# A hybrid decoder layer on one core: the FFN chunk's epilogue in four steps instead of three, and the order of the last down projection

## The chip, the cores and the metric

One NeuronCore of a Trainium2 chip runs the whole program in one launch. The metric is the device time of one execution in microseconds (us); for the kernel before it is 1596.26 us, the median of three runs (1596.19 to 1596.4).

## The reference, cut to what matters

One layer with a model width of 2048 over 256 tokens, in float32: a hybrid mixer, then the FFN on which the change works, then a last norm. D_FF is 5632.

```
h = h + hybrid_mixer(rms_norm(h, norm_mix), ...)
u = rms_norm(h, norm_ffn)
h = h + (silu(u @ w_gate) * (u @ w_up)) @ w_down      # 2048 -> 5632 -> 2048
return rms_norm(h, norm_final)
```

## The kernel before, in words

**Matmuls in halves.** Every float32 operand is cut into a high and a low part by `split` (L107 on ACT makes the high part, L108 on DVE subtracts it from the value), and every product is three matmuls (high by high, low by high, high by low). So each 2048-column piece of a weight costs ACT one activation and DVE one subtraction before PE may use it.

**Units, and who sets the order.** The order is written out by hand: the program issues instructions in the order in which Python runs, and each engine works its own queue in that order. `run` goes through a list of units. For unit j it first issues the cuts (`split`) and the weight loads of units some places ahead, bounded by a count of buffers (`cap`), then `unit.multiply()`, then the unit's epilogue if it is the last of its group (`g.after`), and then it advances `clock` by one and lets `step_side` resume one side job. A side job is a generator: `beside(gen, after, lag)` sets its first step `after` ticks ahead, and after each `yield` it sleeps `lag` ticks. All that a step issues stands in the engines' queues between the matmuls of unit j and those of unit j + 1.

**The FFN's chunks.** D_FF is worked in 11 chunks of 512 columns, in four parts: `PARTS` is (0,3), (3,6), (6,9), (9,11). A chunk (`swiglu`) computes the gate and the up product together in 11 units, in the order N, N, Wp, Ws, N, Wp, Ws, N, Wp, Ws, N. An N unit is 24 matmuls of 512 columns, Wp 9 and Ws 12. All are of line L381. The products are summed in seven PSUM banks (of eight), from which VectorE puts the four results together (`squares_early` after the last Ws, L388 to L390; `squares_end`, L397 to L401). The cut of a Wp also makes four sums on DVE (L363 to L365).

**The chunk's epilogue** is the side job `finish`. It has three steps. Step 1: `squares_end` and two silu activations on ACT (L872). Step 2: two multiplications on DVE (L875, one per 128 tokens) that make act, then four transposes of act on PE (L881, each 128 by 128, into one fresh bank), and the `split` of that bank into the slot `act[f]`. Step 3: the other four transposes into another bank, and their `split`. For a chunk that is not the last of its part `after` is 2, so step 1 stands behind the first unit of the next chunk (N), step 2 behind the second (N) and step 3 behind the third (Wp). For the last chunk of a part `after` is 1: step 1 stands right behind its own last unit, and step 2 and step 3 behind the first two units of the down projection.

**The down projection** follows each part: `down(part, n)` for four groups of 512 output columns. A unit is a K-tile of one chunk's 512 rows, 24 matmuls (L275, L276, L280), so a group has as many units as the part has chunks. It accumulates in two banks. Groups put together in a tuple are interleaved by `in_order`: first all their units but the last one, then the last units. In all parts the first two groups are such a tuple. The last unit of a group uses the part's last chunk. The last part also scales by the final norm (`after`, L916 to L919) and its fourth group is staggered: its two units are worked per token tile, and `final_norm` writes out.

Of the kernel before, what the change touches and what calls it, by code (L numbers as in the profile page):

```python
# [17 lines left out]
D_MODEL = 2048  # L18
# [14 lines left out]
CH = 512  # L33
# [17 lines left out]
def trunk(ctx: ExitStack, tc: tile.TileContext, x, norm_mix, norm_ffn, w_in, w_pool, pool_scale,  # L51
# [19 lines left out]
    def name(s):  # L71
        uid[0] += 1
        return f"{s}_{uid[0]}"

    def slot(shape, dt=F32):
        return slots.tile([P] + shape, dt, tag="slot", name=name("slot"))
# [15 lines left out]
    def bank():  # L92
        return psum.tile([P, CH], F32, tag="bank", name=name("bank"))
# [4 lines left out]
    def cols(n):  # L98
        return slice(n * CH, (n + 1) * CH)
# [4 lines left out]
    def split(hi, lo, src, scale=None):  # L104

        if scale is None:
            nc.scalar.activation(hi, src, AF.Copy)  # L107
            nc.vector.tensor_tensor(lo, src, f32(hi), OP.subtract)  # L108
        else:
            nc.scalar.activation(hi, src, AF.Copy, scale=scale)  # L110
            nc.vector.scalar_tensor_tensor(lo, src, scale, f32(hi), OP.mult, OP.subtract)
# [61 lines left out]
    def square_sum(dst, src):  # L173
        nc.scalar.activation(wk(), src, AF.Square, accum_out=dst)
# [21 lines left out]
    def beside(gen, after=2, lag=2):  # L196
        side.append([clock[0] + after, lag, gen])
# [187 lines left out]
    def squares_early(b):  # L385

        c12, w, x = wk(), wk(), wk()
        nc.scalar.activation(c12, b[1], AF.Copy)  # L388
        nc.vector.tensor_tensor(w, b[6], c12, OP.subtract)
        nc.vector.tensor_tensor(x, b[7], w, OP.add)  # L390
        return c12, w, x

    def squares_end(b, early):

        c12, w, x = early
        c21 = wk()
        nc.vector.tensor_tensor(w, b[5], w, OP.add)  # L397
        nc.vector.tensor_tensor(c21, b[5], x, OP.add)
        nc.vector.tensor_tensor(w, b[3], w, OP.add)  # L399
        nc.vector.tensor_tensor(c12, b[2], c12, OP.add)  # L400
        nc.vector.tensor_tensor(x, b[4], x, OP.subtract)  # L401
        return (w, c12), (c21, x)
# [137 lines left out]
    def qkv(s, base, then):  # L540
        return ([heads_T("q" + s, base, c, HEAD_DIM ** -0.5, turned=s == "a") for c in range(2)]
                + [heads_T("k" + s, base + WIDTH, c, 1.0) for c in range(2)]
                + [tokens("v" + s, base + 2 * WIDTH, c, then if c else None) for c in range(2)])
# [153 lines left out]
    def pair(t):  # L697
        return t.rearrange("p (k s) -> p k s", k=2)
# [154 lines left out]
    def load_gf():  # L853
        gf.append(slot([D_MODEL]))
        nc.sync.dma_start(gf[0], bass.AP(tensor=norm_final.tensor, offset=norm_final.offset,
                                         ap=[[0, P], [1, D_MODEL]]))

    def swiglu(f, last):

        early = []  # L860

        def load(raw, p):
            for i, w in enumerate((w_gate, w_up)):
                nc.sync.dma_start(raw[:, :, i, :], w[2 * p * P:2 * (p + 1) * P, cols(f)].rearrange("(j p) c -> p j c", p=P))

        def begin(b):
            early.append(squares_early(b))

        def finish(b):
            c = squares_end(b, early[0])  # L870
            for t in range(NT):
                nc.scalar.activation(c[t][0], c[t][0], AF.Silu, scale=rstd2[t])  # L872
            yield
            for t in range(NT):
                nc.vector.scalar_tensor_tensor(c[t][1], c[t][1], rstd2[t], c[t][0], OP.mult, OP.mult)  # L875
            act[f] = a = slot([8, SEQ], F32R)
            for k in range(2):
                pt = bank()
                for i in range(2):
                    for t in range(NT):  # L880
                        nc.tensor.transpose(pt[:, i * SEQ + t * P:i * SEQ + (t + 1) * P],  # L881
                                            c[t][1][:, (2 * k + i) * P:(2 * k + i + 1) * P], ident)
                split(a[:, 2 * k:2 * k + 2, :], a[:, 4 + 2 * k:6 + 2 * k, :], pair(pt))
                if k == 0:
                    yield
            ready.add(f)

        def before():
            cap[0] = 9

        def after(b):
            beside(finish(b), after=1 if last else 2, lag=1)

        return Squares(lambda: hT[0], FFN_KINDS, load, after, begin, before)

    def down(part, n):
        f0, f1 = PARTS[part]
        last = part == len(PARTS) - 1
        cs = cols(n)

        def lhs():
            def tile(kt):
                assert kt // 4 in ready
                return act[kt // 4][:, kt % 4, :], act[kt // 4][:, 4 + kt % 4, :]
            return tile

        def before():
            if last and n == 0:
                load_gf()
                nc.scalar.preload_act_table(AF.Sqrt)  # L910

        def after(acc, t=None, c=slice(0, CH)):
            if t is not None:
                return final_norm(acc, t, c)
            for t in range(NT):
                nc.vector.tensor_add(h[t][:, cs], acc[t], h[t][:, cs])  # L916
                if last:
                    square_sum(st3[:, t, n:n + 1], h[t][:, cs])
                    nc.vector.tensor_mul(h[t][:, cs], h[t][:, cs], gf[0][:, cs])  # L919
            if last and n == 2:  # L920
                nc.vector.tensor_reduce(st3[:, :, 4], st3[:, :, 0:3], AX.X, OP.add)
                nc.vector.tensor_scalar(st3[:, :, 4], st3[:, :, 4], 1.0 / D_MODEL, EPS, OP.mult, OP.add)

        return Group(lhs, range(4 * f0, 4 * f1), w_down, f0 * CH, n * CH, after, before, staggered=last and n == 3,
                     span=4)

    def final_norm(acc, t, c):

        hc = h[t][:, 3 * CH + c.start:3 * CH + c.stop]
        a = [st3[:, t, k:k + 1] for k in range(10)]  # L930
        nc.vector.tensor_add(hc, acc[:, c], hc)
        nc.scalar.activation(wk()[:, c], hc, AF.Square, accum_out=a[3])
        nc.vector.tensor_mul(hc, hc, gf[0][:, 3 * CH + c.start:3 * CH + c.stop])
        if c.stop < CH:
            nc.vector.scalar_tensor_tensor(a[4], a[3], 1.0 / D_MODEL, a[4], OP.mult, OP.add)
            return
        nc.scalar.activation(a[6], a[3], AF.Sqrt, scale=1.0 / D_MODEL, bias=a[4])
        nc.vector.scalar_tensor_tensor(a[5], a[3], 1.0 / D_MODEL, a[4], OP.mult, OP.add)
        nc.vector.reciprocal(a[7], a[6])
        nc.vector.scalar_tensor_tensor(a[8], a[7], a[7], a[5], OP.mult, OP.mult)  # L940
        nc.vector.tensor_scalar(a[8], a[8], -0.5, 1.5, OP.mult, OP.add)
        nc.vector.tensor_mul(a[9], a[7], a[8])
        for n in (0, 1, 3, 2):
            hn = h[t][:, cols(n)]
            if n in (0, 3):
                nc.vector.tensor_scalar(hn, hn, a[9], None, OP.mult)
            else:
                nc.scalar.activation(hn, hn, AF.Copy, scale=a[9])
            nc.sync.dma_start(out[toks(t), cols(n)], hn)

    groups = qkv("a", 0, start_block)
# [5 lines left out]
    for part, (f0, f1) in enumerate(PARTS):  # L957
        for f in range(f0, f1):
            groups += [swiglu(f, f == f1 - 1)]
        groups += [(down(part, 0), down(part, 1)), down(part, 2), down(part, 3)]  # L960

    def first_norm():
        rstd_of(st1)
# [39 lines left out]
```

## Time and profile before

| | |
|---|---|
| median of three runs | 1596.26 us |
| the profiled execution's own time | 1599.63 us |
| its span, first to last instruction | 1597.9 us |
| mean granted TensorE clock | 0.993 |
| PE busy (matmuls) | 1563.4 us, 98% |
| PEld busy (weight loads) | 1332.2 us, 83% |
| DVE busy | 1000.1 us, 63% |
| ACT busy | 724.8 us, 45% |
| DMA | mean 188 GB/s |

The span is the time between the first and the last instruction of one profiled execution. PE and PEld are the two sides of TensorE: matmuls and the weight loads ahead of them. Where a row ends in square brackets, these hold the time for which the engine sat idle just before it, and what ended the wait. The matmuls of the FFN's first chunk begin at 850.3 us; from there to the end of the span chunks and down projections follow each other.

### The profile page before, as it was taken

The numbers are of one execution on the slowest core, as the hardware profiler recorded it, in microseconds if no ns is written. First come the engines' busy times: TensorE is split into PE (matmuls) and PEld (weight loads), VectorE is DVE, ScalarE is ACT, GpSimd is POOL, SyncE is SP. The second block draws the span as 40 slices with busy tenths as digits, with TensorE's granted clock in tenths as the row PEclk, the third lists the DMA queues.
The fourth block names the chain that finished last, engine by engine and source line by source line (L and its number), as shares of the span: only waits on it lengthen the run. The fifth ranks groups of instructions, "written<-read, shape, count | busy, mean of one in ns | idle before, by whom it ended". The sixth has DMA issues, their size and how long they took to land.

```text
span 1597.9 us, 19167 instructions
## 1 busy us (share of the span) xinstructions
PE 1563.4 (98%) x7921; PEld 1332.2 (83%) x7921; DVE 1000.1 (63%) x996; ACT 724.8 (45%) x754; POOL 26.4 (2%) x94
## 2 busy tenths in 40 slices
PE   8999999999999999999999899999999999999997
PEld 8998999988888888888888777888778887788876
DVE  6453664735464453644657788576885768857675
ACT  7324443445644344343555455343553445534453
POOL 2000000101000000000000000000000000000000
PEclk9999999999999999999999999999999999999999
DMA  9655454554555555567555456555565555755551
GB/s 344 211 185 181 148 167 158 191 176 140 190 193 197 183 187 185 184 209 252 175 181 181 162 183 237 163 179 186 183 237 168 176 187 182 236 185 174 195 211 53
DMA packets 152359, 300.12 MB, mean 188 GB/s; under 512 B 6432, under 2 KB 7504, under 8 KB 152144
## 3 DMA queue, kind: packets, MB, share of 16 engines
q1 hardware_dynamic: 151968, 297.84, 55.3%
q8 instruction: 62, 1.02, 0.3%
q0 software_dynamic: 304, 1.06, 0.2%
q14 instruction: 25, 0.20, 0.0%
HBM read 296.77 MB, written 2.11 MB: 187 GB/s over the span
## 4 chain that ended last, share of the span: by engine, by line
PE 86%; DVE 8%; ACT 3%; issue 2%; DMA 0%; ACTq 0%; SPq 0%; DVEq 0%
PE bank L381 19%; PE bank L275 17%; PE bank L276 17%; PE bank L280 16%; PE bank L295 5%; PE bank L297 5%; PE bank L303 5%; DVE slot L108 4%; ACT slot L107 2%; DVE wk L875 1%; PE bank L881 1%; DVE slot L363 1%; ACT wk L872 1%; DVE wk L399 0%; DVE wk L397 0%
## 5 line engine op out<-in xcount | busy, mean ns | idle before, releaser
L108 DVE TENSOR_TENSOR slot<-slot,slot 128x1024 fp32r<-128x1024 f32 (+3 forms) x459 | 700.6, 1563 | 277.7 <-ACT slot L107 277.7
L107 ACT ACTIVATE slot<-slot 128x1024 fp32r<-128x1024 f32 (+3 forms) x459 | 590.3, 1328 | 336.7 <-DVE slot L108 122.6
L275 PE MATMUL bank<-slot,slot 128*128 128x512 f32 (+1 forms) x1192 | 466.9, 392 | 0.0
L276 PE MATMUL bank<-slot,slot 128*128 128x512 f32 (+1 forms) x1192 | 464.4, 390 | 0.0
L280 PE MATMUL bank<-slot,slot 128*128 128x512 f32 (+1 forms) x1192 | 310.2, 388 | 0.0
L381 PE MATMUL bank<-slot,slot 128*128 128x512 f32 x1254 | 293.0, 393 | 0.0
L381 PEld LDWEIGHTS bank<-slot,slot 128*128 128x128 f32 x1254 | 235.5, 189 | 49.1 <-DVE slot L108 0.7
L275 PEld LDWEIGHTS bank<-slot,slot 128*128 128x128 f32 x1192 | 225.5, 189 | 45.7
L276 PEld LDWEIGHTS bank<-slot,slot 128*128 128x128 f32 x1192 | 225.5, 189 | 45.6
L280 PEld LDWEIGHTS bank<-slot,slot 128*128 128x128 f32 x1192 | 222.9, 188 | 46.0
L381 PE MATMUL bank<-slot,late 128*128 128x512 f32 x759 | 173.8, 389 | 0.0
L381 PEld LDWEIGHTS bank<-slot,late 128*128 128x128 f32 x759 | 142.5, 188 | 29.6
L295 PE MATMUL bank<-slot,slot 128*128 128x256 f32 x640 | 159.3, 287 | 0.2 <-ACT slot L107 0.2
L297 PE MATMUL bank<-slot,slot 128*128 128x256 f32 x640 | 157.5, 283 | 0.0
L295 PEld LDWEIGHTS bank<-slot,slot 128*128 128x128 f32 x640 | 123.2, 193 | 0.7 <-ACT slot L107 0.6
L297 PEld LDWEIGHTS bank<-slot,slot 128*128 128x128 f32 x640 | 123.3, 193 | 0.0
L107 ACT ACTIVATE slot<-bank 128x512 fp32r<-128x512 f32 (+1 forms) x46 | 23.2, 523 | 155.9 <-PE bank L881 80.6
L303 PE MATMUL bank<-slot,slot 128*128 128x256 f32 x640 | 89.8, 283 | 0.0
L303 PEld LDWEIGHTS bank<-slot,slot 128*128 128x128 f32 x640 | 82.6, 192 | 0.0
L108 DVE TENSOR_TENSOR slot<-bank,slot 128x512 fp32r<-128x512 f32 (+1 forms) x46 | 26.8, 596 | 60.8 <-ACT slot L107 60.8
L755 ACT ACTIVATE wk<-bank,st 128x512 f32<-128x512 f32 x24 | 15.2, 686 | 85.6 <-PE bank L280 85.6
L916 DVE TENSOR_TENSOR slot<-bank,slot 128x512 f32<-128x512 f32 x30 | 19.6, 686 | 44.7 <-PE bank L280 44.7
(156 smaller groups left out, 575.4 us busy)
## 6 DMA issues: line engine op xcount, KB each, us to landing
slot<-in_w_in_dram SPq DMA_DIRECT2D x103, 1024.0 KB, 5.1
slot<-in_w_gate_dram SPq DMA_DIRECT2D x88, 512.0 KB, 3.9
slot<-in_w_up_dram SPq DMA_DIRECT2D x88, 512.0 KB, 4.8
slot<-in_w_down_dram SPq DMA_DIRECT2D x44, 1024.0 KB, 5.1
slot<-in_w_out_dram SPq DMA_DIRECT2D x16, 1024.0 KB, 5.1
slot<-in_w_br_a_dram SPq DMA_DIRECT2D x8, 1024.0 KB, 5.1
slot<-in_w_br_b_dram SPq DMA_DIRECT2D x8, 1024.0 KB, 5.1
slot<-in_w_br_c_dram SPq DMA_DIRECT2D x8, 1024.0 KB, 5.1
```

The costliest lines, as they stand in the source:

```text
L107: nc.scalar.activation(hi, src, AF.Copy)
L108: nc.vector.tensor_tensor(lo, src, f32(hi), OP.subtract)
L275: nc.tensor.matmul(acc[:, c], hi[:, toks(t)], whi[:, j, c], start=i + j == 0, stop=False)
L276: nc.tensor.matmul(acc[:, c], lo[:, toks(t)], whi[:, j, c], start=False, stop=False)
L280: nc.tensor.matmul(acc[:, c], hi[:, toks(t)], wlo[:, j, c], start=False, stop=i + j == n - 1)
L295: nc.tensor.matmul(o, whi[:, j, w], hi, start=i + j == 0 and c % 2 == 0, stop=False, skip_group_check=True)
L297: nc.tensor.matmul(o, whi[:, j, w], lo, start=False, stop=False, skip_group_check=True)
L303: nc.tensor.matmul(o, wlo[:, j, w], hi, start=False, stop=i + j == n - 1 and c % 2 == 1, skip_group_check=True)
L363: nc.vector.tensor_tensor(s[:, 0:2], raw[:, 0:1].to_broadcast([P, 2, CH]), raw[:, 1:3], OP.add)
L381: nc.tensor.matmul(g.banks[b], x[:, s, :], w[:, k, :], start=start, stop=g.left[b] == 0)
L872: nc.scalar.activation(c[t][0], c[t][0], AF.Silu, scale=rstd2[t])
L916: nc.vector.tensor_add(h[t][:, cs], acc[t], h[t][:, cs])
```

## The change

A `yield` is put into `finish` between the two multiplications and the first transposes. The epilogue has four steps: `squares_end` and silu; the multiplications; four transposes with their split; the other four with theirs. With the lag of one tick both sets of transposes, the slot of act and the two splits stand one unit later in the queues. For a chunk inside a part they stand behind the third unit (Wp) and the fourth (Ws) of the next chunk, for the last chunk of a part behind the second and the third unit of the down projection.

In the last part, which has two chunks, three down groups instead of two are put in the tuple, so their order of units is group 0, 1, 2 of the first chunk, then group 0, 1, 2 of the second chunk, and then the staggered fourth group. In the parts of three chunks the order of units stays.

```
             for t in range(NT):
                 nc.vector.scalar_tensor_tensor(c[t][1], c[t][1], rstd2[t], c[t][0], OP.mult, OP.mult)
+            yield
             act[f] = a = slot([8, SEQ], F32R)
             for k in range(2):
                 pt = bank()
...
         for f in range(f0, f1):
             groups += [swiglu(f, f == f1 - 1)]
-        groups += [(down(part, 0), down(part, 1)), down(part, 2), down(part, 3)]
+        k = 2 if f1 - f0 > 2 else 3
+        groups += [tuple(down(part, n) for n in range(k))] + [down(part, n) for n in range(k, D_MODEL // CH)]
```

## Rows read from the trace of the kernel before

**Rows 1.** The page, part 1: busy time, share of the span, instructions per engine.

```profile
PE 1563.4 (98%) x7921; PEld 1332.2 (83%) x7921; DVE 1000.1 (63%) x996; ACT 724.8 (45%) x754; POOL 26.4 (2%) x94
```

**Rows 2.** Groups by line, PE, 890 to 1598: busy us, mean ns, idle before, releaser.

```profile
L381 PE MATMUL bank<-slot,slot 128*128 128x512 f32 x1140 | 266.0, 393 | 0.0
...
L881 PE MATMUL bank<-ident,wk 128*128 128x128 f32 x88 | 17.5, 304 | 19.0 <-DVE wk L875 19.0
```

**Rows 3.** Timeline of PE behind the first chunk: start, length, instructions, idle before.

```profile
908.40 0.47 PE L881 MATMUL bank<-ident,wk 128*128 128x128 f32 x1 [4.22 <-DVE wk L875]
909.06 0.90 PE L881 MATMUL bank<-ident,wk 128*128 128x128 f32 x3 [0.19 <-DVE wk L875]
909.61 4.19 PE L381 MATMUL bank<-slot,slot 128*128 128x512 f32 x9
913.60 1.05 PE L881 MATMUL bank<-ident,wk 128*128 128x128 f32 x4
```

**Rows 4.** Timeline of PE behind the second, the fourth and the fifth chunk.

```profile
954.88 0.33 PE L881 MATMUL bank<-ident,wk 128*128 128x128 f32 x1 [0.65 <-DVE wk L875]
955.55 0.55 PE L881 MATMUL bank<-ident,wk 128*128 128x128 f32 x3 [0.33 <-DVE wk L875]
955.85 2.32 PE L381 MATMUL bank<-slot,slot 128*128 128x512 f32 x9
958.00 0.60 PE L881 MATMUL bank<-ident,wk 128*128 128x128 f32 x4
...
1111.07 0.55 PE L881 MATMUL bank<-ident,wk 128*128 128x128 f32 x3 [0.33 <-DVE wk L875]
...
1154.41 0.33 PE L881 MATMUL bank<-ident,wk 128*128 128x128 f32 x1 [0.81 <-DVE wk L875]
```

**Rows 5.** Timeline of PE behind the third chunk, and the last.

```profile
994.89 0.33 PE L881 MATMUL bank<-ident,wk 128*128 128x128 f32 x1 [2.25 <-DVE wk L875]
...
1547.63 0.33 PE L881 MATMUL bank<-ident,wk 128*128 128x128 f32 x1 [2.25 <-DVE wk L875]
```

**Rows 6.** Stretches: length, busy of PE, PEld, DVE, ACT, POOL, then PEclk, DMA, GB/s.

```profile
996.00:1001.00 5.00, 5.00 (x17) 3.92 (x17) 2.98 (x2) 2.40 (x2) 0.00 (x0) 0.66 0.51 193
1195.00:1200.00 5.00, 4.89 (x17) 4.06 (x18) 2.21 (x3) 2.40 (x2) 0.00 (x0) 0.69 0.60 211
1394.00:1399.00 5.00, 4.67 (x23) 3.86 (x23) 2.56 (x3) 2.40 (x2) 0.00 (x0) 1.00 0.61 210
1548.00:1554.00 6.00, 5.70 (x20) 4.59 (x21) 3.23 (x3) 2.40 (x2) 0.00 (x0) 0.72 0.01 3
...
908.00:914.00 6.00, 5.42 (x15) 4.14 (x16) 1.70 (x3) 0.60 (x1) 0.00 (x0) 0.50 0.08 12
...
1113.90:1155.40 41.50, 40.35 (x182) 33.00 (x179) 36.84 (x30) 21.44 (x15) 0.00 (x0) 1.00 0.60 203
```

**Rows 7.** Timeline of PE and DVE in the last down projection.

```profile
1553.95 2.00 PE L280 MATMUL bank<-slot,slot 128*128 128x512 f32 x8
...
1557.06 0.69 DVE L108 TENSOR_TENSOR slot<-bank,slot 128x512 fp32r<-128x512 f32 x1 [3.46 <-ACT slot L107]
...
1559.89 1.98 PE L280 MATMUL bank<-slot,slot 128*128 128x512 f32 x8
...
1565.33 1.98 PE L280 MATMUL bank<-slot,slot 128*128 128x512 f32 x8
```

**Rows 8.** Timeline of DVE and ACT behind the fourth chunk.

```profile
1109.60 1.41 DVE L875 SCALAR_TENSOR_TENSOR wk<-wk,st,wk 128x512 f32<-128x512 f32 x2
...
1111.71 0.60 ACT L107 ACTIVATE slot<-bank 128x512 fp32r<-128x512 f32 x1 [4.35 <-PE bank L881]
1112.34 0.69 DVE L108 TENSOR_TENSOR slot<-bank,slot 128x512 fp32r<-128x512 f32 x1 [1.33 <-ACT slot L107]
...
1115.40 1.22 DVE L363 TENSOR_TENSOR slot<-slot 128x1024 f32<-128x1024 f32 x1
...
1120.11 4.49 DVE L108 TENSOR_TENSOR slot<-slot,slot 128x2048 fp32r<-128x2048 f32 x2 [0.38 <-ACT slot L107]
```

More of the change, by code (lines that the diff above doesn't have):

```diff
@@ L875, in finish @@
                 nc.vector.scalar_tensor_tensor(c[t][1], c[t][1], rstd2[t], c[t][0], OP.mult, OP.mult)
+            yield
             act[f] = a = slot([8, SEQ], F32R)
@@ L959, in trunk @@
             groups += [swiglu(f, f == f1 - 1)]
-        groups += [(down(part, 0), down(part, 1)), down(part, 2), down(part, 3)]
+        k = 2 if f1 - f0 > 2 else 3
+        groups += [tuple(down(part, n) for n in range(k))] + [down(part, n) for n in range(k, D_MODEL // CH)]
     def first_norm():
```

## The prediction

> **What bounds the kernel now.** I read the page's busy times first: PE is busy for 98% of the span, DVE for 63% [rows 1], so time can be won only where PE stands idle or runs slowly. The groups by line over the FFN come next. There the chunks' matmuls (L381) have 0.0 us of idle time before them, and one group holds what PE waits for: the transposes of act at L881, 19.0 us, released by the multiplications at L875 [rows 2]. PE takes its queue in order, so it stands still although the next unit's weights lie ready. Last I read PE's timeline at each of the 11 chunks, because the average hides that the stalls have three sizes.
>
> Behind the first chunk PE waits 4.22 us and then 0.19 for the second multiplication [rows 3]. Behind the second it waits 0.65 + 0.33, behind the fifth and the eighth 0.81 + 0.34 each, and behind the fourth, seventh and tenth, which follow a down projection, 0.33 alone [rows 4]. Behind the last chunk of each part (third, sixth, ninth, eleventh) it is 2.25 (the first and the last of four in [rows 5]) and 0.34 for the second multiplication, as at the other chunks. Together 4.41 + 0.98 + 2 x 1.15 + 3 x 0.33 + 4 x 2.59 = 19.0, which is the group's sum.
>
> There is a second cost. Right behind three of the four stalls of 2.25 us the granted clock falls: its mean is 0.66, 0.69 and 0.72 over stretches of 5, 5 and 6 us, and 1.00 behind the ninth chunk, where the stall was as long [rows 6]. Time lost in them: 5 x 0.34 + 5 x 0.31 + 6 x 0.28 = 1.70 + 1.55 + 1.68 = 4.9 us. Behind the first chunk the mean is 0.50 over 6 us, that is the lower of the two levels, 1.2 GHz. Nine matmuls take 913.60 - 909.61 = 3.99 us there [rows 3], against 958.00 - 955.85 = 2.15 us for the same nine behind the second chunk [rows 4]; at half speed over the 5.42 us for which PE was busy [rows 6] it lost 2.7 us.
>
> **The change part by part.** *The stalls inside a part.* No instruction is added; eight transposes, two copies and two subtractions per chunk move behind one more unit. A full unit of 24 matmuls takes 1565.33 - 1559.89 = 5.44 us, 0.227 us per matmul [rows 7]. For chunks 1, 2, 4, 5, 7, 8 and 10 the unit that comes ahead is a Wp, 9 x 0.227 = 2.04 us. The multiplications keep their place in DVE's queue, so they end when they end now. Behind the second, fourth, fifth, seventh, eighth and tenth chunk the whole wait is at most 0.81 + 0.34 = 1.15 us, under 2.04: all of it goes, 0.98 + 2.30 + 0.99 = 4.27 us. At the first chunk 4.22 - 2.04 = 2.18 us stay, and the 0.19 for the second multiplication stays too: 2.04 us are won.
>
> *The stalls at the end of a part.* The unit that comes ahead is 5.44 us of down's matmuls against a wait of 2.59: all four go, 10.36 us. Idle time won in sum: 4.27 + 2.04 + 10.36 = 16.7 us.
>
> *The clock.* With the stalls of 2.25 us gone I let the 4.9 us behind them go as well. The first chunk keeps a stall of 2.18, about as long as those that cost 1.6 us each where the clock fell and nothing where it didn't; I take 1.6 of its 2.7 as staying, so 1.1 go (bounds 0 and 2.7). In sum 6.0 us, with bounds of 0 and 7.6. The low bound is the case that the clock falls without regard to the stall; what speaks against it is that no stretch of the FFN without a long stall that I read shows less than full clock.
>
> The Trainium skill, page "TensorE: Matmul & The Clock Gate", section "What's actually happening", says that the throttled state is the default and that activity releases it. By that rule the slow stretches go where PE stops idling, and the sum has its 6.0 us; without it the sum is 16.7. The trace agrees at four stalls and not at a fifth: behind the ninth chunk the clock stayed at 1.00 after the same 2.25 us.
>
> *What is late next.* (a) DVE and ACT. Behind the fourth chunk the multiplications end at 1111.0, then come the copy at 1111.71 and the subtraction at 1112.34, each after waiting for PE [rows 8]. Now the first split still stands right behind the multiplications in both queues (no cut is issued between these steps, the next Wp and Ws cuts come behind it), and the second split moves behind these two cuts. So the cuts that PE needs start one split earlier than now as counted in DVE's queue; the wait for PE that holds them is for the first transposes (after Wp) and no more for the second (now also after Wp): the same place in PE's queue. I cost it at nothing. In the down projections the first split waits a unit longer and holds one cut, but units are cut four ahead, 4 x 5.44 us, and DVE has only about 2.3 us of cut per unit (half of the 4.49 of two [rows 8]). If that cover were gone, the price would be one cut of 2.3 us per chunk.
>
> (b) PSUM. A chunk opens banks in the order N (four), Wp (one), Ws (two), and two more go to the transposes: nine for eight. Before, the ninth was Ws's, now it is that of the second transposes: they need the first transposes' bank back. That takes copy and subtraction, from 1111.71 to 1113.03, 1.3 us [rows 8], and Ws lies between with 12 x 0.227 = 2.72 us. Free by 1.4 us; cost 0, and at most the rival's price below.
>
> (c) down's last K-tile needs both splits. In parts of three chunks a unit of 5.44 us stands between the second transposes and the first reader. In the last part none does, before and after: now 1559.89 - 1553.95 = 5.94 us from one unit's last eight matmuls to the next's, of which 5.44 are the unit and the other 0.50 are the four transposes and the start behind them [rows 7]. The split ends at 1557.06 + 0.69 = 1557.75, and the readers of its half come eight matmuls, 1.8 us, behind the unit's start. The third group put into the tuple keeps this; without it the readers would stand one unit too early. It also moves three epilogues next to each other, 5.44 us apart, with about 2.8 us of DVE each (four operations of 0.69, the time of one 512-column operation [rows 8]): they fit; at worst the last one is late by a split, 0.7 us. Weight loads of that part change places in SP's queue among themselves; the pace of 5.44 us shows that PE waits for none there now.
>
> **Sum.** 16.7 + 6.0 = 22.7 us. Against the profiled execution: a span of 1597.9 - 22.7 = 1575.2, and 1599.63 - 22.7 = 1576.9 with the 1.7 around it. That execution is 3.4 us above the median of the runs; I take the same 22.7 off the median: 1573.6 us.
>
> **Rivals.** *A: DVE becomes the bound inside the parts.* From 1113.9 to 1155.4 it is busy for 36.84 of 41.5 us, 89% [rows 6], and PE's small waits may be what lets it keep up. Then the 4.27 us of the second to tenth chunk come back as waits at a cut, and the clock's gain may be halved: 16.7 - 4.3 + 3 = 15.4, 1580.9 us. For it: the share. Against it: weight matmuls wait 0.0 us now [rows 2], and the 4.7 us left over per chunk are more than the 1.15 that the stall gives at most.
>
> *B: slower, the ninth bank.* If DVE reaches the first split only behind the cuts of Wp and Ws, the second transposes find no bank, and all of PE waits behind them. Price: the cut of Wp and the Ws behind it run from 1115.40 to 1122.4, 7.0 us [rows 8]; with the split's 1.3 and less Ws's 2.72 that is 5.6 us, in seven chunks 39 us: 1573.6 + 39 = 1612.6. It decides from the point where the split ends over 2.72 us behind the first transposes. Against it: the order in the queue, where the split stands ahead of those cuts.
>
> *C: it does nothing.* The bubbles are for want of a buffer, and the transposes wait in the new place as in the old: 1596 us. The Trainium skill, page "Perfetto Trace Analysis", section "Optimization Strategy", says that the same gap repeating on the engine that should be saturated can mean too little SBUF or PSUM. The trace differs: the first transposes start when the first multiplication has ended and the next three 0.67 us later, at the pace of L875 (1.41 us for two [rows 8]), and the wait is of three sizes.
>
> **Chances.** The forecast (1570 to 1577) 0.62; A, or some other part of the gain that stays out (1577 to 1586), 0.25; C 0.06; B or another new wait that costs more than is won 0.07. A measurement of this kernel tells 0.2%, 3.2 us, from no change. So faster 0.87, same 0.06, slower 0.07. The range of 8 in 10 is 1570 to 1583: its low end takes 26 us off, that is all 19.0 idle and nearly all the clock's 7.6, its high end lies 3.3 us over the case in which the clock gives nothing back (1596.3 - 16.7 = 1579.6).
>
> **What would show it.** Right: PE's idle time before L881 falls from 19.0 to about 2.4 us, all at the first chunk; the granted clock stays at 1.00 behind the third, sixth and eleventh chunk; weight matmuls still wait 0.0. Wrong: idle time before L381 or L275 (A), idle time before L881 released by the subtraction L108 (B) or by L875 again in every chunk (C), or slow stretches of the clock without a stall.

## The result, and the profile after

The changed kernel takes 1573.91 us (median of four runs, 1573.71 to 1574.4) against 1596.22 for the kernel before, measured beside it (1595.57 to 1596.4). The ratio is 0.9861, with a 95% interval of 0.9844 to 0.9878: 22.3 us less. The forecast was 1573.6. Of the executions reported under Experiments one stands apart: of the kernel with the later transposes at the parts' last chunks alone one of five took 3838.08 us, for a cause that isn't known, and the other four took 1582.98 to 1583.62.

The page of the changed kernel, part 1 (busy us, share of the span, instructions), which answers to [rows 1]:

```profile
span 1572.3 us, 19167 instructions
...
PE 1554.3 (99%) x7921; PEld 1329.4 (85%) x7921; DVE 999.1 (64%) x996; ACT 724.0 (46%) x754; POOL 27.4 (2%) x94
```

As many instructions as before, and the same work on DVE and ACT. PE's busy time is 9.1 us shorter although it does the same matmuls. The rows of the transposes alone are 3.7 us shorter (17.5 us in [rows 2], 13.8 below), mostly because a transpose that waits by itself has a longer row than one in a stream; the rest ran in part at a higher clock.

The groups by line on PE over the FFN, from 845 us on (busy us, mean ns, idle time before, releaser). The transposes are line L882 now, and these rows answer to [rows 2]:

```profile
L381 PE MATMUL bank<-slot,slot 128*128 128x512 f32 x1254 | 292.3, 392 | 0.0
...
L882 PE MATMUL bank<-ident,wk 128*128 128x128 f32 x88 | 13.8, 278 | 2.5 <-DVE wk L875 2.5
```

Of 19.0 us of idle time 2.5 are left, and the weight matmuls still wait for nothing. PE's timeline behind the first, the second and the ninth chunk shows where; it answers to [rows 3 to 5]:

```profile
909.33 0.33 PE L882 MATMUL bank<-ident,wk 128*128 128x128 f32 x1 [2.22 <-DVE wk L875]
909.99 0.90 PE L882 MATMUL bank<-ident,wk 128*128 128x128 f32 x3 [0.33 <-DVE wk L875]
910.54 4.33 PE L381 MATMUL bank<-slot,slot 128*128 128x512 f32 x12
914.72 0.60 PE L882 MATMUL bank<-ident,wk 128*128 128x128 f32 x4
...
953.97 0.60 PE L882 MATMUL bank<-ident,wk 128*128 128x128 f32 x4
954.32 3.00 PE L381 MATMUL bank<-slot,slot 128*128 128x512 f32 x12
...
1377.72 1.99 PE L280 MATMUL bank<-slot,slot 128*128 128x512 f32 x8
1379.54 0.60 PE L882 MATMUL bank<-ident,wk 128*128 128x128 f32 x4
1379.90 0.48 PE L275 MATMUL bank<-slot,slot 128*128 128x512 f32 x1
```

Only the first chunk keeps a stall, of 2.22 + 0.33 us (2.18 + 0.19 were forecast). Everywhere else the four transposes are one row without a wait. The stretches (length, busy of PE, PEld, DVE, ACT, POOL, granted clock, DMA share, GB/s) behind the first and the third chunk answer to [rows 6]:

```profile
910.00:916.00 6.00, 6.00 (x23) 4.99 (x24) 4.37 (x5) 3.10 (x3) 0.00 (x0) 0.72 0.28 103
...
994.00:1000.00 6.00, 6.00 (x30) 4.98 (x29) 3.11 (x3) 2.40 (x2) 0.00 (x0) 1.00 0.52 175
```

Behind the first chunk the clock still falls, to a mean of 0.72 where it was 0.50; behind the third it stays at 1.00.

### The profile page after: what moved, and what is told of

Read it like the earlier page. It is cut to its first block, busy times and chain, and to the rows that moved or that the text cites. A ratio compares the mean times of both kernels' runs of the same rounds, so it can differ in the third digit from the quotient of the medians.

```text
span 1572.3 us, 19167 instructions
## 1 busy us (share of the span) xinstructions
PE 1554.3 (99%) x7921; PEld 1329.4 (85%) x7921; DVE 999.1 (64%) x996; ACT 724.0 (46%) x754; POOL 27.4 (2%) x94
## 4 chain that ended last, share of the span: by engine, by line
PE 97%; DVE 1%; ACT 0%; DMA 0%; issue 0%; SPq 0%; ACTq 0%
PE bank L381 28%; PE bank L275 17%; PE bank L276 17%; PE bank L280 17%; PE bank L295 5%; PE bank L297 5%; PE bank L303 5%; PE bank L882 1%; DVE slot L108 1%; PE bank L551 0%; PE bank L180 0%; DMA slot<-in_x_dram 0%; ACT slot L107 0%; PE bank L835 0%; PE bank L552 0%
## 5 line engine op out<-in xcount | busy, mean ns | idle before, releaser
L108 DVE TENSOR_TENSOR slot<-slot,slot 128x1024 fp32r<-128x1024 f32 (+3 forms) x459 | 701.2, 1563 | 269.8 <-ACT slot L107 269.7
L108 DVE TENSOR_TENSOR slot<-bank,slot 128x512 fp32r<-128x512 f32 (+1 forms) x46 | 26.7, 595 | 48.3 <-ACT slot L107 48.3
```

## What the count of idle time left out

The two profiled spans differ by 25.6 us, the medians by 22.3, and the idle time by 16.5. To see what a stall costs, I read starts against starts. These are PE's rows around the ninth chunk's first transposes in the kernel before, where the clock did not fall:

```profile
1389.50 1.97 PE L280 MATMUL bank<-slot,slot 128*128 128x512 f32 x8
1393.73 0.33 PE L881 MATMUL bank<-ident,wk 128*128 128x128 f32 x1 [2.25 <-DVE wk L875]
1394.39 0.55 PE L881 MATMUL bank<-ident,wk 128*128 128x128 f32 x3 [0.34 <-DVE wk L875]
1394.69 0.48 PE L275 MATMUL bank<-slot,slot 128*128 128x512 f32 x1
```

From the start of the last eight matmuls to the next unit's first it is 1394.69 - 1389.50 = 5.19 us; in the changed kernel 1379.90 - 1377.72 = 2.18. The stall cost 3.01 us, and its idle time was counted as 2.25 + 0.34 = 2.59. The missing 0.42 is in the rows' lengths. A matmul's shown end lies past the point at which the next could have started: in a stream the rows are 0.39 us long and start 0.227 apart. And a transpose that waits alone is shown 0.33 long, while four that follow each other take 0.36 together. The same over the whole third part, from the first matmul behind one down projection to the first behind the next, where the clock did not fall in either kernel; the kernel before:

```profile
1257.24 4.92 PE L381 MATMUL bank<-slot,slot 128*128 128x512 f32 x21
...
1455.16 5.15 PE L381 MATMUL bank<-slot,slot 128*128 128x512 f32 x22
```

and the changed kernel:

```profile
1242.31 19.88 PE L381 MATMUL bank<-slot,slot 128*128 128x512 f32 x87
...
1434.91 25.32 PE L381 MATMUL bank<-slot,slot 128*128 128x512 f32 x111
```

197.92 us against 192.60: 5.32 won, where the idle time in that part was 0.33 + 1.15 + 2.59 = 4.07. So the idle column gave about three quarters of what the stalls cost.

Each chunk can be read in this way, from the last matmul ahead of its first four transposes to the first one behind them. The changed kernel wins 2.0 us behind the first chunk, 1.4 behind the second, 0.7 behind the fourth, seventh and tenth, 1.6 behind the fifth and eighth and 3.0 behind the last chunk of each of the four parts: 2.0 + 1.4 + 3 x 0.7 + 2 x 1.6 + 4 x 3.0 = 20.7 us. The extra time that a slow clock gives these few rows is left out of it.

## Experiments

All kernels were timed in alternation with the kernel before, whose medians in the three sets were 1596.37, 1597.17 and 1597.29 us. Differences to "before" are to the set's own median, differences to "the changed kernel" to 1573.91.

### One part alone: the last part's order

```
-            yield
             act[f] = a = slot([8, SEQ], F32R)
```

(from the changed kernel: the yield is taken out, the tuple of three stays)

> The kernel before with the last part's order alone (three down groups in the tuple), the epilogue left in three steps. Theory (the gain is the stalls of PE ahead of the transposes, and they go because the transposes stand a unit later): no transposes move, so all 19.0 us of idle time before them stay and the time stays at 1596.2, within 3 us. Rival (the new order of the last part gives a part of the 22.3 us by itself): faster by over 3 us, and idle time before the transposes behind the last chunk under 2.59 us.

Measured: 1596.55 us, ratio 1.0002 (0.9993 to 1.0011). PE's idle time before the transposes is 19.1 us. The order of the last part gives nothing by itself; it only makes room for the later transposes.

### One part alone: the chunks inside a part, and the parts' last chunks

```
+            if not last:          # first kernel; `if last:` in the second
                 yield
```

(the first has the old order in the last part, the second the new one)

> The later transposes for the seven chunks inside a part alone; the last chunks of the parts and the last part's order as before. Theory: the idle time of the inner chunks goes (4.27 us) and 2.04 us of the first chunk's, and about 1.1 us of slow clock behind the first chunk: 7.4 us in all, 1588.8. The four stalls of 2.59 us and the slow clock behind three of them stay. Rival (VectorE bounds the inner chunks): 4.27 us come back as waits at the weight matmuls, and only about 3 us are won, 1593.

> The later transposes for the last chunks of the four parts alone, with the last part's new order; the inner chunks as before. Theory: 4 x 2.59 = 10.4 us of idle time and 4.9 us of slow clock behind it go: 15.3 us, 1580.9; the idle time before the transposes falls from 19.0 to 8.6 us. With the inner run the two gains add up to the whole. Rival (the clock falls without regard to the stalls): 10.4 us alone, 1585.8.

Measured: 1589.71 us (0.9959, 0.9947 to 0.9972) for the inner chunks and 1583.01 (0.9918, 0.9904 to 0.9931) for the parts' last, 6.7 and 13.4 us. The idle time left before the transposes is 12.8 and 8.7 us, so each half takes away its own stalls and no wait comes elsewhere: no sign of DVE as the bound. The second half lies between what the theory and its rival expected, 1580.9 and 1585.8; it fits the reading by starts, 4 x 3.01 = 12.0 us and little of the clock. The first half gave less than the 20.7 - 12.0 = 8.7 us that the reading by starts leaves it, and the two do not add up to the whole, 20.0 us against 22.3. The granted clocks of the runs show where that went: the mean is 0.996 in the fastest run (1586.96 us), 0.995 in the next two (1589.69 and 1589.71) and 0.993 in the slowest (1591.14 and 1591.62), while 18 of the 21 runs of the kernel before in this set have 0.996. So the half won its stalls and lost a part again to more slow clock; why the clock fell more often there stays open. The profile of the fastest shows a slow stretch behind the third and the sixth chunk, as [rows 6] do.

### The stalls kept, but filled with matmuls

```
                 pt = bank()
+                if k == 0:
+                    fx = hT[0].pairs[0]
+                    for r in range(19 if f == 0 else 10 if last else 3 if f % 3 else 0):
+                        nc.tensor.matmul(pt, fx[:, 0, :], fx[:, 0:4].rearrange("p a s -> p (a s)"), start=True, stop=True)
```

> The kernel before with its waits kept and filled: ahead of the first transposes PE gets matmuls of 512 columns into the bank that the transposes then overwrite, 19 behind the first chunk (4.3 us for its wait of 4.22), 10 behind the last chunks of the parts (2.27 for 2.25) and 3 behind the second, fifth and eighth (0.68 for 0.65 to 0.81). So the transposes start when they start now, and only what PE does in the wait changes. The results are those of the reference. Theory (the clock falls because PE idles): the slow stretches behind the first, third, sixth and eleventh chunk go, 2.7 + 4.9 = 7.6 us, 1588.6. Rival (the clock falls there for another reason): 1596.2 and the same slow stretches.

Measured: 1593.11 us, ratio 0.9979 (0.9970 to 0.9988): 3.3 us, less than half of what I expected, but more than none. PE's timeline at the third chunk:

```profile
989.15 1.98 PE L280 MATMUL bank<-slot,slot 128*128 128x512 f32 x8
990.96 2.43 PE L882 MATMUL bank<-slot 128*128 128x512 f32 x10
993.38 0.33 PE L885 MATMUL bank<-ident,wk 128*128 128x128 f32 x1
994.04 0.55 PE L885 MATMUL bank<-ident,wk 128*128 128x128 f32 x3 [0.33 <-DVE wk L875]
994.34 0.47 PE L275 MATMUL bank<-slot,slot 128*128 128x512 f32 x1
```

and the stretch behind the first chunk (columns as above):

```profile
890.00:930.00 40.00, 39.67 (x179) 32.49 (x178) 33.58 (x30) 17.98 (x15) 0.00 (x0) 1.00 0.49 162
```

The ten matmuls end where the transposes may start, and from a unit's last eight matmuls to the next unit's first it is 994.34 - 989.15 = 5.19 us, as at the ninth chunk of the kernel before: the wait is as long. The clock stays at 1.00 behind all 11 chunks. So the clock fell because PE stood idle. The rule of the Trainium skill that the prediction weighed ("TensorE: Matmul & The Clock Gate", "What's actually happening": activity releases the throttle) agrees with this run.

What was off is the price. In the timed runs of the kernel before, the slow stretches cost 3.3 us, and 7.6 in the one profiled execution on which I counted: that execution took 1599.63 us, 3.4 over the median. The granted clocks agree: 18 of the 21 timed runs of the kernel before have a mean of 0.996 and the filled kernel's all 0.998 or 0.999, which is 0.002 x 1596 = 3.2 us; the profiled execution had 0.993, as only one of the 21 did. The profile of the kernel with the last part's order alone, whose stalls are the same, shows slow stretches behind the first and the third chunk and none behind the sixth and the last. Its stretches around the third, the sixth and the last chunk:

```profile
960.00:1010.00 50.00, 47.44 (x207) 38.79 (x206) 38.85 (x30) 24.82 (x17) 0.00 (x0) 0.97 0.60 204
1185.00:1210.00 25.00, 22.41 (x102) 18.14 (x102) 14.96 (x13) 11.42 (x9) 0.00 (x0) 1.00 0.49 169
1535.00:1575.00 40.00, 37.42 (x169) 30.57 (x168) 23.93 (x24) 15.73 (x18) 0.00 (x0) 1.00 0.14 54
```

Which stalls lower the clock changes from run to run.

### The last stall filled, and the last stall moved

```
+                if k == 0 and f == 0:     # ten matmuls into pt, as above
...
-            yield
+            for _ in range(2 if f == 0 else 1):
+                yield
```

(two kernels, each from the changed one)

> The changed kernel with its last stall, behind the first chunk, filled by 10 matmuls of 512 columns (2.27 us) into the bank that the transposes then overwrite. Theory (the slow clock there comes of the idle time): the slow stretch goes and nothing else, at most 1.7 us as in the profile: 1572.2 to 1573.9. Rival (the clock falls there anyway): 1573.9 and the same slow stretch. With the first-chunk run it parts the stall's idle time from its clock.

> The changed kernel with one more yield behind the first chunk alone, so its transposes stand behind Ws as well (12 matmuls, 2.7 us later). Theory (a stall goes when the unit put ahead is longer than the wait): the 2.22 and 0.33 us that are left behind the first chunk go, and with them the slow stretch there, 1.7 us in the profile: 2.5 to 4.7 us faster than the changed kernel, 1569.2 to 1571.4. Rival (VectorE's lag behind the first chunk comes out at the next weights instead): idle time before the weight matmuls of about 2 us and no gain, 1574.

Measured: 1571.98 us filled (0.9841, 0.9827 to 0.9854), 1.9 less than the changed kernel and 0.2 under the range expected. Its clock stays at 1.00 from 890 to 930 us:

```profile
890.00:930.00 40.00, 39.67 (x179) 32.52 (x178) 35.39 (x31) 19.78 (x16) 0.00 (x0) 1.00 0.51 169
```

So about 1.9 us of slow clock were left in the changed kernel. With 3.3 before, the change has won back about 1.3 us of clock. This is good to some 0.7 us only, because the two kernels were timed in different sets: the runs of the kernel before with a mean clock of 0.996 have medians of 1596.31, 1596.85 and 1596.18 us in the three sets.

One unit later the time is 1571.21 us (0.9835, 0.9821 to 0.9848), 2.7 less than the changed kernel. PE's timeline behind the first chunk:

```profile
908.82 0.82 PE L883 MATMUL bank<-ident,wk 128*128 128x128 f32 x4
909.39 5.74 PE L381 MATMUL bank<-slot,slot 128*128 128x512 f32 x24
916.62 0.66 PE L883 MATMUL bank<-ident,wk 128*128 128x128 f32 x4 [1.49 <-DVE slot L108]
```

The first transposes wait no more, but the second do, 1.49 us, for a subtraction. The time is in the theory's range, at its upper end, but a wait is left that neither theory named; it is the rival of the ninth bank in small. Behind Ws the first split stands in DVE's queue behind the cuts of Wp and Ws, and the second transposes wait for its bank. The next run makes that wait in every inner chunk.

### The ninth bank

```
+                if k == 0 and not last:
+                    yield
                 split(a[:, 2 * k:2 * k + 2, :], a[:, 4 + 2 * k:6 + 2 * k, :], pair(pt))
-                if k == 0:
+                if k == 0 and last:
                     yield
```

> The changed kernel with the first split of the inner chunks moved from behind the first transposes to a unit later, so it stands behind the cuts of Wp and Ws in ACT's and DVE's queues; the second transposes and their split follow it at once. Theory (the ninth bank: the second transposes need the bank of the first, and wait for its split): PE waits at the second transposes in all seven inner chunks, 3.2 us each where the cuts start as soon as the multiplications end, up to 5.6 where they start as late as now, 22 to 39 us in all, and slow clock behind some of them: 1596 to 1613, idle time before the transposes released by L108. Rival (PSUM has a bank to spare there): no wait, 1574.

Measured: 1604.67 us, ratio 1.0039 (1.0027 to 1.0052) to the kernel before, 30.8 us over the changed kernel. The group of the transposes over the FFN:

```profile
L882 PE MATMUL bank<-ident,wk 128*128 128x128 f32 x88 | 15.2, 298 | 22.5 <-DVE slot L108 20.0 <-DVE wk L875 2.5
```

and the timeline of DVE and PE behind the fourth chunk:

```profile
1110.73 1.41 DVE L875 SCALAR_TENSOR_TENSOR wk<-wk,st,wk 128x512 f32<-128x512 f32 x2
1112.06 1.22 DVE L363 TENSOR_TENSOR slot<-slot 128x1024 f32<-128x1024 f32 x1
...
1116.80 2.29 DVE L108 TENSOR_TENSOR slot<-slot,slot 128x2048 fp32r<-128x2048 f32 x1 [0.40 <-ACT slot L107]
1119.00 0.68 DVE L108 TENSOR_TENSOR slot<-bank,slot 128x512 fp32r<-128x512 f32 x1
1119.74 1.12 PE L882 MATMUL bank<-ident,wk 128*128 128x128 f32 x4 [2.93 <-DVE slot L108]
```

The second transposes start when the first split's subtraction has ended at 1119.68, seven times, 2.9 us each as idle time. The mean granted clock of the span is 0.991 against 0.998. So the rival's mechanism is real, and what keeps the changed kernel clear of it is the order in DVE's queue: there the first split stands ahead of the two cuts.

### The multiplications moved instead

The first chunk's stall goes back to DVE. In the changed kernel DVE and ACT do this behind the first chunk:

```profile
903.14 1.34 ACT L872 ACTIVATE wk<-wk,st 128x512 f32<-128x512 f32 x2 [4.16 <-DVE wk L399]
903.62 0.68 DVE L401 TENSOR_TENSOR wk<-bank,wk 128x512 f32<-128x512 f32 x1
906.32 2.29 DVE L108 TENSOR_TENSOR slot<-slot,slot 128x2048 fp32r<-128x2048 f32 x1 [2.01 <-ACT slot L107]
908.53 1.41 DVE L875 SCALAR_TENSOR_TENSOR wk<-wk,st,wk 128x512 f32<-128x512 f32 x2
```

The multiplications (L875) stand behind a cut whose subtraction (L108) waits 2.01 us for ACT, while silu (L872) has ended at 904.48. Two kernels put them ahead of it; the one from the changed kernel, the other from the kernel before.

```
-            yield
             for t in range(NT):
                 nc.vector.scalar_tensor_tensor(c[t][1], c[t][1], rstd2[t], c[t][0], OP.mult, OP.mult)
+            yield
```

> The changed kernel with the two multiplications moved into the first step, right behind silu and ahead of the next cut in DVE's queue; the transposes stay where the change put them. In the changed kernel DVE idles 2.01 us ahead of that cut's subtraction (906.32 behind the first chunk), for ACT's copy; silu ends at 904.48, so the multiplications can run from 904.5 to 905.9 in this gap. Theory (the wait is the length of DVE's queue ahead of the multiplications): the last stall, behind the first chunk, goes with its slow clock, and no new wait comes: 3 to 4.7 us under the changed kernel, 1569.2 to 1571. Rival (DVE, waiting for silu, holds the cut back and PE waits for its weights): idle time before weight matmuls, 1574 or more.

> The kernel before with the multiplications moved into the first step and nothing else: three steps, the transposes one unit earlier than in the changed kernel, the last part's order as before. Theory: the multiplications end about 4 us earlier than before the change, more than every stall but the first chunk's 4.22 + 0.19 (silu ends at 903.55 there, the transposes are due at 904.18, so about 0.7 us stay): 1569 to 1572, as fast as the changed kernel or faster without a later place for the transposes. Rival (only a later place in PE's queue takes the stalls away): over 1585.

Measured: 1569.34 us (1569.17 to 1570.07; 0.9827, 0.9814 to 0.9841) from the changed kernel, and 1570.49 (1569.21 to 1570.66; 0.9833, 0.9819 to 0.9846) from the kernel before. The timeline of DVE, ACT and PE behind the first chunk in the first of them:

```profile
903.90 1.41 DVE L874 SCALAR_TENSOR_TENSOR wk<-wk,st,wk 128x512 f32<-128x512 f32 x2
904.07 1.90 ACT L107 ACTIVATE slot<-slot 128x2048 fp32r<-128x2048 f32 x1
906.00 2.29 DVE L108 TENSOR_TENSOR slot<-slot,slot 128x2048 fp32r<-128x2048 f32 x1 [0.69 <-ACT slot L107]
906.71 0.60 PE L882 MATMUL bank<-ident,wk 128*128 128x128 f32 x4
```

its group of the transposes over the FFN:

```profile
L882 PE MATMUL bank<-ident,wk 128*128 128x128 f32 x88 | 13.2, 272 | 0.0
```

and the timeline behind the first chunk in the second:

```profile
903.25 1.41 DVE L874 SCALAR_TENSOR_TENSOR wk<-wk,st,wk 128x512 f32<-128x512 f32 x2
904.05 0.33 PE L881 MATMUL bank<-ident,wk 128*128 128x128 f32 x1
904.72 0.55 PE L881 MATMUL bank<-ident,wk 128*128 128x128 f32 x3 [0.33 <-DVE wk L874]
```

The multiplications fill the time in which DVE waited for ACT's copy anyway, and the cut's subtraction starts no later. With them early the three steps are enough: PE's idle time before the transposes is 0.3 us in the second kernel. The two medians are 1.2 us apart, but the runs overlap and both profiled spans are 1567.5 us: that the later place, the fourth step and the last part's new order still give something is not shown. Both kernels beat the changed one, by 4.6 and 3.4 us between the medians; the first is 28 us under its own "before".

## Why the prediction was right, and which of its terms were not

- **What bounds the kernel** held: PE's stalls ahead of the transposes, released by L875. Each half alone moved the time, doing the last part's order alone did not, and earlier multiplications took the same stalls away without moving a transpose.
- **Which stalls go** held chunk by chunk. All of the second to eleventh chunk's went, and behind the first 2.22 + 0.33 us stayed, near the 2.18 + 0.19 of the working. "All at the first chunk" was seen.
- **The size of the stalls** was too small. The step "Idle time won in sum: 16.7 us" added up the idle column. That column did fall by 16.5, but a stall costs more than its idle time: 5.32 us against 4.07 in the third part. Taking the clock's 1.3 us off the 22.3 leaves 21.0 us for the stalls; read by starts chunk by chunk they come to 20.7.
- **The clock's share** was too large. The step "In sum 6.0 us" took slow stretches from one execution, and one that was 3.4 us slower than the median, with a mean clock of 0.993 where most runs have 0.996; then it was taken off the median. The filled stalls show 3.3 us in the timed runs, of which about 1.9 stay behind the first chunk: about 1.3 won back. The bounds stood at 0 and 7.6 and held it.
- The two errors, 4.3 us too little and 4.7 too much, cancel. The sum of 22.7 against 22.3 is nearer than its terms, and that nearness is luck.
- **What is late next** held in the points that the traces show: the second transposes have their bank in time (0.0 us before them), the weight matmuls wait for nothing, the last part's units keep their pace. That the third group in the tuple is needed was argued from the code alone and not tried.
- **Rival A** (DVE as the bound) fell: idle time before the weight matmuls is 0.0 with the whole change and with either half. **Rival B** was ruled out by the order in the queue, as argued, and its mechanism was shown: 2.9 us per chunk where it was forecast at 5.6, because the cuts ahead of the split start at the multiplications' end and no more behind the first split. **Rival C** fell.
- Two readings of the working are off and change nothing in the sum: the subtraction at 1112.34 waited 1.33 us for ACT's copy, and only the copy for PE [rows 8]; and the range's high end lies 3.4 us, not 3.3, over 1579.6.
- What I did not see is the cheaper cause: the wait was the length of DVE's queue ahead of the multiplications, with a gap of 2.01 us in it. The rows for it were there; I asked how late the transposes may come, and not why the multiplications were late.

## What to carry to other kernels

When an in-order engine stalls on a small operation of an epilogue, first look at what stands ahead of its producer on the producer's own queue: putting the producer into a gap there took away all the stalls but 0.3 us, and moving the consumer back only those that are shorter than the unit put ahead of it. Moving a consumer later also moves what frees its buffers; count the banks that are open at its new place. Price a stall from start to start against an undisturbed pass, and don't take a clock loss from a single execution.

## What the hardware showed that was not expected

Stalls of the same 2.25 us on PE lowered the granted clock in some places and some runs and not in others: of the four parts' last chunks, behind the third, sixth and eleventh but not the ninth in the profile of the kernel before, and behind the third alone in the profile with the last part's order alone. Filling the waits with matmuls kept the clock at 1.00 everywhere and made a kernel with 68 more matmuls 3.3 us faster.
